# Down projections of an encoder trunk: eight pairs by Strassen's rule, and low parts of weights from an adding transfer

## The chip, the cores and the metric

The kernel runs on one core of one Trainium2 chip. Its time is the time on the device in microseconds (us), the median of several executions. A profile of one more execution shows what each engine did: TensorE (PE; its weight loads are PEld), VectorE (DVE), ScalarE (ACT), GpSimd (POOL), SyncE (SP, which only issues transfers here), and the 16 DMA engines.

## What is computed

A two-layer encoder trunk on 256 tokens of width 2048, in float32. Each layer is a token mixer (attention) and a gated channel mixer. Only the second one's last product is touched, the down projection, which takes 5632 channels back to 2048:

```python
D_MODEL, SEQ, D_FF = 2048, 256, 5632

def conv_glu(h, w_up, conv_w, conv_b, w_down):
    u = h @ w_up
    gate, val = u[..., :D_FF], u[..., D_FF:]
    gate = depthwise_conv3(gate, conv_w, conv_b)
    return (jax.nn.gelu(gate, approximate=False) * val) @ w_down

for i in range(2):
    h = rms_norm(x, p['mix_pre'])
    m = mixer_dilated_gqa(h, ...) if i == 0 else mixer_mla(h, ...)
    x = x + rms_norm(m, p['mix_post'])
    h = rms_norm(x, p['ffn_pre'])
    x = x + rms_norm(conv_glu(h, *p['ffn']), p['ffn_post'])
```

## The kernel before

**Products in three parts.** TensorE multiplies float32 in a rounded form (`F32R`). To keep float32's precision, each operand is split into a high part (the value rounded) and a low part (what the rounding lost), and each product is made of three: high by high, high by low, low by high. The weights are split on the way: a chunk of 128 x 1024 floats (512 KB; two blocks of 128 rows by 512 columns) is loaded by SP into a tile `raw` (four buffers), ACT copies it into `whi`, which rounds it (line 173), and DVE subtracts `whi` from `raw` into `wlo` (line 174). `whi` and `wlo` have three buffers each (lines 167, 168).

**The chunk planner.** All weights of the program stand in one list of chunks. `weights()` hands out the next chunk, splits the chunks up to two places further on (`i + 3` is the end of the range that is split, line 191), and issues the loads of up to three more. So a chunk's split is written into the program two chunks before its use, and its buffers come free when the chunk three places ahead of it has been multiplied. The recording layer then orders each engine's instructions itself; what stands on an engine is therefore shown below as rows of the built program.

**The down projection** (`down`, from line 1002 on) runs once for each layer, and covers the 2048 columns in two halves of 1024 (`h`). A half takes 22 pairs of 128-row blocks. A *plain* pair is two chunks, one for each 512 columns; a chunk is multiplied in 12 matmuls of 128 x 512: for each of the two groups of 128 tokens four with `whi` (lines 1101 and 1102) and then two with `wlo` (line 1104). A *Strassen* pair treats tokens, rows and columns as a 2 x 2 by 2 x 2 block product and needs seven products in place of eight, so 21 matmuls in place of 24. Its weights go through four items in place of two chunks: item 0 is the tile `seven_a` as loaded, then DVE makes four sums and differences of half tiles (`Seven.sums`, line 76) from `seven_a` and `seven_b`, which change `seven_a` and `seven_b` in place and write `seven_t`; items 1, 2 and 3 are the changed `seven_a`, `seven_b` and `seven_t` (the last is half as long). Each item is split on ACT and DVE as any chunk is. Items 0, 1 and 2 feed six matmuls each, item 3 three. `seven_a`, `seven_b` and `seven_t` have one buffer each, so the next pair's load waits until this pair's items are split.

**Order.** `down_order` sets the order of items in a half: some plain chunks ahead (`LEAD`: five in the first half, one in the second), then for each Strassen pair its four items with four plain chunks between them (item 0, plain, plain, item 1, plain, items 2 and 3, plain), and what is left of the plain chunks at the end. Sums of the tokens' side are made once for each layer by `sums()`, on DVE and ACT, and kept in `seven0` to `seven2`.

Of the kernel before, what the change touches and what calls it, by code (L numbers as in the profile page):

```python
# [9 lines left out]
F32 = mybir.dt.float32  # L10
F32R = mybir.dt.float32r
BF16 = mybir.dt.bfloat16
AF = mybir.ActivationFunctionType
ALU = mybir.AluOpType
AX = mybir.AxisListType

P = 128
# [7 lines left out]
EPS = 1e-6  # L25
NEG = -1e30
HOLD = 3
LAGS = 3, 2, 1

XM = 0, 1, 3, 2  # L30

PAIRS = 6
LEAD = 5, 1


def down_order(h):

    plain = [("plain", p, o) for o in range(2) for p in range(PAIRS, KF // 2)]  # L40
    out, plain = plain[:LEAD[h]], deque(plain[LEAD[h]:])
    for p in range(PAIRS):
        for j in (0, None, None, 1, None, 2, 3, None):
            out.append(plain.popleft() if j is None else ("seven", p, j))
    return out + list(plain)


class Seven:
# [5 lines left out]
    def __init__(self, a, b):  # L54
        self.srcs, self.raw = (a, b), None
# [31 lines left out]
class Model:  # L87
# [60 lines left out]
    def _load(self, i):  # L148
        if i >= len(self.chunks) or i in self.loaded or i < self.at or i in self.made:
            return  # L150
        if isinstance(self.chunks[i], tuple):
            self.chunks[i][0].load(self)
            self.loaded[i] = None
            return
        raw = self.wp.tile([P, 1024], F32, tag="raw", name="raw", bufs=4)
        self.nc.sync.dma_start(out=raw, in_=self.chunks[i])
        self.loaded[i] = raw

    def _split(self, i, parts=1):
        if i >= len(self.chunks) or i in self.made:  # L160
            return
        self._load(i)
        raw = self.loaded.pop(i)
        seven, step = self.chunks[i] if raw is None else (None, 0)
        if seven:
            raw = seven.step(self, step)
        hi = self.wp.tile([P, 1024], F32R, tag="whi", name="whi", bufs=3)
        lo = self.wp.tile([P, 1024], F32R, tag="wlo", name="wlo", bufs=3)
        n = raw.shape[-1] // parts
        with self.behind(self.gate):  # L170
            for j in range(parts):
                s = slice(n * j, n * j + n)
                self.nc.scalar.copy(hi[:, s], raw[:, s])  # L173
                self.nc.vector.tensor_tensor(out=lo[:, s], in0=raw[:, s], in1=hi[:, s].bitcast(F32),  # L174
                                             op=ALU.subtract)
        if seven and step == 0:
            seven.sums(self)
        self.made[i] = (hi, lo)
# [8 lines left out]
    def weights(self, upto=None):  # L187

        i = self.at
        if upto is None:  # L190
            upto = i + (2 if self.lead else 3)
            self.follow()
        for j in range(i, upto):
            self._split(j)
        for j in range(upto, i + 6):
            self._load(j) if j < upto + 4 else None
        self.at += 1
        return self.made.pop(i)
# [191 lines left out]
    def out_proj(self, nk, parts, post, pre, m3, order=None, before={}):  # L390
# [27 lines left out]
        part = self.three(ss)  # L418
        ps = self.proj_tok(nk, parts, order, hold=HOLD)
        m.append(room.tile([P, 2, 512], F32, tag=tag, name="m3", bufs=bufs))  # L420
# [103 lines left out]
    def attend(self, scores, sc, mask, v, v_gen, put, sp):  # L524
# [31 lines left out]
        for i in range(2):  # L556
            nc.vector.tensor_scalar(out=p[:, i, :], in0=p[:, i, :], scalar1=den[:, i:i + 1], scalar2=None,
                                    op0=ALU.mult)
        for _ in range(LAGS[0]):
            yield  # L560
# [9 lines left out]
        use["p"] -= 1  # L570
        for _ in range(LAGS[1]):
            yield
# [28 lines left out]
    def turned(self, sp, ps, n, block, tab, put, scale=None):  # L601
# [4 lines left out]
        for t in range(2):  # L606
# [25 lines left out]
            yield  # L632
        for _ in range(LAGS[2]):
            yield
# [367 lines left out]
    def down(self, gh, gl, post, pre):  # L1002

        nc = self.nc
# [3 lines left out]
        seven, m, gains = [], [], []  # L1008

        def sums():  # L1010

            for i in range(PAIRS // 2):
                tmp = self.act.tile([P, 2, 1024], F32, tag="xm3", name="sums")
                add(tmp[:, 0], gh[i].rearrange("p k t -> p (k t)").bitcast(F32),
                    gl[i].rearrange("p k t -> p (k t)").bitcast(F32))
                a = tmp[:, 0].rearrange("p (q k t f) -> p q k t f", q=2, k=2, t=2)
                s = tmp[:, 1].rearrange("p (q n f) -> p q n f", q=2, n=4)
                a11, a12, a21, a22 = (a[:, :, k, t] for t in range(2) for k in range(2))
                add(s[:, :, 0], a21, a22)
                add(s[:, :, 1], s[:, :, 0], a11, ALU.subtract)  # L1020
                add(s[:, :, 2], a11, a21, ALU.subtract)
                add(s[:, :, 3], a12, s[:, :, 1], ALU.subtract)
                yield
                seven.append(self.act.tile([P, 2, 4, 2, P], F32R, tag=f"xm{i}", name=f"seven{i}"))
                self.parted(seven[i][:, :, :, 0, :], seven[i][:, :, :, 1, :], s)
                yield

# [47 lines left out]

        gains.append(self.gain_row(post, 0))
        self.now(sums())
        ended = None
        for h in range(2):
            items = down_order(h)  # L1080
            units = [n for n, item in enumerate(items) if item[0] == "seven"]
            if h == 0:
                gains.append(self.gain_row(post, 1))
            n = len(items) - (HOLD if h else 0)
            todo = [(i, t) for i in range(n) for t in range(2)] + \
# [9 lines left out]
            def products(i, t, w):  # L1095
                group = []
                while used and used[0][1][:2] == (i, t):
                    q, (_, _, b, x, blk) = used.popleft()
                    group.append((banks[b], *x(), slice(512 * blk, 512 * blk + 512), q == first[b], q == last[b]))
                for bank, xh, xl, c, start, _ in group:  # L1100
                    mm(bank, xh, w[0][:, c], start=start, stop=False)  # L1101
                    mm(bank, xl, w[0][:, c], start=False, stop=False)  # L1102
                for bank, xh, _, c, _, stop in group:
                    mm(bank, xh, w[1][:, c], start=False, stop=stop)  # L1104

            for i in range(n):
                if i == units[0]:
                    banks += [self.psum("at") for _ in range(4)]
                w = self.weights()
# [17 lines left out]
        part = self.three(ss)  # L1127
        ws = [self.weights(self.at + HOLD - j) for j in range(HOLD)]
        for t in range(2):
            for j in range(HOLD):  # L1130
                products(n + j, t, ws[j])
# [24 lines left out]
    def all_chunks(self):  # L1156
        a = self.a
        groups = lambda w, gs: [w[g, c] for g in gs for c in range(w.shape[1])]
        out = groups(a["w_in0"], [8, 6, 7, 0, 2, 4, 1, 3, 5])
        out += [a["w_out0"][g, c] for g in range(4) for c in (4, 5, 6, 7, 0, 1, 2, 3)]  # L1160

        def down(w):
            items = []
            for h in range(2):
                pairs = [Seven(w[2 * h, p], w[2 * h + 1, p]) for p in range(PAIRS)]
                items += [w[2 * h + j, p] if kind == "plain" else (pairs[p], j) for kind, p, j in down_order(h)]
            return items

        ffn = lambda l: groups(a[f"w_up{l}"], [g for j in range(NFG) for g in (j, NFG + j)]) + \
            down(a[f"w_down{l}"])  # L1170
        out += ffn(0)
        out += groups(a["w_in1"], [0, 1]) + [a["w_kr"]]
        for p in range(8):
            out += groups(a["w_qr"], [p // 4]) if p % 4 == 0 else []
            out += [a["w_qn"][p], a["w_kn"][p]]
            out += groups(a["w_v"], [p // 2]) if p % 2 == 0 else []
        out += groups(a["w_out1"], range(4))
        out += ffn(1)
        return out
# [67 lines left out]
```

## Time and profile before

| | us |
|---|---|
| Median of 3 runs | 2062.15 (2062.04 to 2062.24) |
| Span of the profiled execution | 2060.1 |
| First to last matmul of layer 0's down projection | 822.75 to 1055.30 |
| The same for layer 1 | 1818.1 to 2050.6 |

The profiled execution's span runs from its first to its last instruction; the median of the runs, which is taken without the profiler, is 2.05 us above it. The two down projections are alike, 1020 matmuls and some 232.6 us each. In the groups of instructions and in the timeline, a row names the line, the engine, the operation and the tiles (what is written, an arrow, what is read); a matmul's duration is modelled and overlaps the next one, so the pace of matmuls is read from their starts.

### The profile page before, as it was taken

How to read it: one execution, taken by the hardware profiler on the slowest of the kernel's cores; microseconds unless marked ns; L12 is line 12 of the kernel's file. 1: busy time of each engine (PE TensorE's matmuls, PEld its weight loads, DVE VectorE, ACT ScalarE, POOL GpSimd, SP SyncE). 2: the span in 40 equal slices, each digit the busy share in tenths (PEclk: the TensorE clock that was granted, in tenths of full speed). 3: DMA queues.
4: the chain of work that ended last, by engine and by line, in shares of the span. 5: the costliest groups of instructions: out<-in, count | busy, mean ns of one | idle time of the engine just before them, and what ended most of it. 6: DMA issues, size and time to landing. Idle time of an engine off the chain costs nothing.

```text
span 2060.1 us, 29196 instructions
## 1 busy us (share of the span) xinstructions
PE 2043.4 (99%) x10905; PEld 1750.0 (85%) x10905; DVE 1478.4 (72%) x2263; ACT 1129.3 (55%) x1753; POOL 0.2 (0%) x4
## 2 busy tenths in 40 slices
PE   9999999999999999999999999999999999999998
PEld 7888888888888888888878998888888888888886
DVE  6877757766766767878787875676766766787877
ACT  6655546555555555555465664555555555554553
POOL 0000000000000000000000000000000000000000
PEclk9999999999999999999999999999999999999999
DMA  8545566666566666566655445566566566556664
GB/s 318 176 153 161 166 197 193 186 194 193 185 194 191 185 194 189 184 211 197 203 179 170 124 134 173 176 210 189 185 193 193 184 195 193 185 184 205 204 206 141
DMA packets 108717, 385.96 MB, mean 187 GB/s; under 512 B 12064, under 2 KB 12576, under 8 KB 108576
## 3 DMA queue, kind: packets, MB, share of 16 engines
q1 hardware_dynamic: 108288, 383.83, 59.3%
q8 instruction: 85, 1.39, 0.3%
q14 instruction: 56, 0.46, 0.1%
q10 hardware_dynamic: 288, 0.28, 0.0%
HBM read 381.96 MB, written 2.10 MB: 186 GB/s over the span
## 4 chain that ended last, share of the span: by engine, by line
PE 96%; DVE 3%; issue 0%; ACT 0%; DMA 0%; DVEq 0%; SPq 0%; ACTq 0%
PE ps L244 31%; PE ps L245 16%; PE ps L230 8%; PE ps L231 8%; PE ps L232 8%; PE ps L1104 7%; PE ps L1101 7%; PE ps L1102 7%; PE ps L537 1%; PE ps L300 1%; DVE x L454 1%; DVE wlo L174 1%; PE ps L478 0%; DVE sums L1005 0%; DMA raw<-in_w_in 0%
## 5 line engine op out<-in xcount | busy, mean ns | idle before, releaser
L174 DVE TENSOR_TENSOR wlo<-raw,whi 128x1024 fp32r<-128x1024 f32 (+1 forms) x662 | 807.6, 1221 | 490.3 <-ACT whi L173 487.6
L173 ACT CAST whi<-raw 128x1024 fp32r<-128x1024 f32 (+1 forms) x662 | 694.3, 1050 | 642.7 <-PE ps L244 302.4
L244 PE MATMUL ps<-xhl,whi 128*128 128x512 f32 x2816 | 978.7, 394 | 1.0 <-DVE xhl L591 1.0
L245 PE MATMUL ps<-xhl,wlo 128*128 128x256 f32 x2816 | 779.2, 277 | 0.0
L244 PEld LDWEIGHTS ps<-xhl,whi 128*128 128x128 f32 x2816 | 527.6, 188 | 123.1 <-DVE xhl L591 2.0
L245 PEld LDWEIGHTS ps<-xhl,wlo 128*128 128x128 f32 x2816 | 528.9, 188 | 1.0 <-DVE wlo L174 0.5
L1101 PE MATMUL ps<-whi,gh 128*128 128x512 f32 x584 | 227.3, 389 | 0.0
L1102 PE MATMUL ps<-whi,gl 128*128 128x512 f32 x584 | 227.2, 389 | 0.0
L1104 PE MATMUL ps<-wlo,gh 128*128 128x512 f32 x584 | 182.0, 390 | 0.8 <-DVE wlo L174 0.8
L230 PE MATMUL ps<-whi,xhl 128*128 128x512 f32 x352 | 138.7, 395 | 0.9 <-ACT whi L173 0.8
L231 PE MATMUL ps<-wlo,xhl 128*128 128x512 f32 x352 | 137.6, 391 | 0.0
L232 PE MATMUL ps<-whi,xhl 128*128 128x512 f32 x352 | 137.2, 390 | 0.0
L1104 PEld LDWEIGHTS ps<-wlo,gh 128*128 128x128 f32 x584 | 109.1, 188 | 25.2 <-DVE wlo L174 2.7
L1101 PEld LDWEIGHTS ps<-whi,gh 128*128 128x128 f32 x584 | 109.6, 188 | 22.8
L1102 PEld LDWEIGHTS ps<-whi,gl 128*128 128x128 f32 x584 | 109.6, 188 | 22.8
L230 PE MATMUL ps<-whi,oh 128*128 128x512 f32 x256 | 100.0, 390 | 0.0
L231 PE MATMUL ps<-wlo,oh 128*128 128x512 f32 x256 | 99.7, 389 | 0.0
L232 PE MATMUL ps<-whi,ol 128*128 128x512 f32 x256 | 99.6, 389 | 0.0
L305 ACT COPY half<-ps 128x256 f32<-128x256 f32 x176 | 65.1, 370 | 43.9 <-PE ps L244 34.6
L230 PEld LDWEIGHTS ps<-whi,xhl 128*128 128x128 f32 x352 | 66.0, 188 | 14.5 <-ACT whi L173 1.1
L232 PEld LDWEIGHTS ps<-whi,xhl 128*128 128x128 f32 x352 | 66.1, 188 | 13.9
L231 PEld LDWEIGHTS ps<-wlo,xhl 128*128 128x128 f32 x352 | 66.3, 188 | 13.4 <-DVE wlo L174 0.9
(211 smaller groups left out, 2061.0 us busy)
## 6 DMA issues: line engine op xcount, KB each, us to landing
raw<-in_w_up SPq DMA_DIRECT2D x352, 512.0 KB, 4.1
raw<-in_w_down SPq DMA_DIRECT2D x128, 512.0 KB, 3.9
raw<-in_w_in SPq DMA_DIRECT2D x88, 512.0 KB, 3.7
raw<-in_w_out SPq DMA_DIRECT2D x64, 512.0 KB, 4.1
seven_a<-in_w_down SPq DMA_DIRECT2D x24, 512.0 KB, 4.5
seven_b<-in_w_down SPq DMA_DIRECT2D x24, 512.0 KB, 4.2
gb<-in_post SPq DMA_DIRECT2D x16, 256.0 KB, 3.8
raw<-in_w_qn SPq DMA_DIRECT2D x8, 512.0 KB, 3.6
```

The source lines that it names most:

```text
L173: self.nc.scalar.copy(hi[:, s], raw[:, s])
L174: self.nc.vector.tensor_tensor(out=lo[:, s], in0=raw[:, s], in1=hi[:, s].bitcast(F32), op=ALU.subtract)
L230: mm(ps, lh, rh, start=start, stop=False)
L231: mm(ps, lh, rl, start=False, stop=False)
L232: mm(ps, ll, rh, start=False, stop=stop)
L244: mm(out[i], hi[:, s], x(k), start=k == 0, stop=False)
L245: mm(out[i][:, :T], lo[:, s], x(k)[:, :T], start=False, stop=k == nk - 1)
L300: self.tc.keep_in_program_order(self.nc.tensor.transpose(out, x, self.ident))
L305: self.nc.scalar.copy(b, ps[:, T:])
L1101: mm(bank, xh, w[0][:, c], start=start, stop=False)
L1102: mm(bank, xl, w[0][:, c], start=False, stop=False)
L1104: mm(bank, xh, w[1][:, c], start=False, stop=stop)
```

## The change

Eight pairs of the 22, no longer six, go by Strassen's rule (`PAIRS`), in both halves and both layers. With fewer plain chunks left, the order between the items is closer: pairs with an even number get two plain chunks between their items, pairs with an odd number three. The fourth tile of token sums, `seven3`, lives in the channel mixer's own pool.

Of the 28 plain chunks of a half, every second one up to the 24th (12 in all) is wrapped in `Summed`. For such a chunk ACT makes `whi` as before, and then writes its negative into `wlo`; a transfer issued by POOL then adds the chunk, read from HBM a second time, to what stands in `wlo`. DVE's subtraction falls away there. `whi` and `wlo` get four buffers, and `weights()` splits one chunk further ahead (`AHEAD`), in the whole program. The space that is set aside for transfers issued by POOL is cut to 1024 bytes a partition.

```diff
+AHEAD = 4
-PAIRS = 6
+PAIRS = 8
     for p in range(PAIRS):
-        for j in (0, None, None, 1, None, 2, 3, None):
+        for j in (0, None, None, 1, None, 2, 3) if p % 2 else (0, None, 1, None, 2, 3):
             out.append(plain.popleft() if j is None else ("seven", p, j))
+class Summed:
+    def __init__(self, src):
+        self.src = src
...
-        hi = self.wp.tile([P, 1024], F32R, tag="whi", name="whi", bufs=3)
-        lo = self.wp.tile([P, 1024], F32R, tag="wlo", name="wlo", bufs=3)
+        hi = self.wp.tile([P, 1024], F32R, tag="whi", name="whi", bufs=AHEAD)
+        lo = self.wp.tile([P, 1024], F32R, tag="wlo", name="wlo", bufs=AHEAD)
+        if isinstance(self.chunks[i], Summed):
+            with self.behind(self.gate):
+                self.nc.scalar.copy(hi, raw)
+                self.nc.scalar.activation(lo, hi.bitcast(F32), AF.Copy, scale=-1.0)
+            self.nc.gpsimd.dma_start(out=lo, in_=self.chunks[i].src, accum_op=ALU.add)
+            self.made[i] = (hi, lo)
+            return
...
-            upto = i + (2 if self.lead else 3)
+            upto = i + (2 if self.lead else AHEAD)
...
-                seven.append(self.act.tile([P, 2, 4, 2, P], F32R, tag=f"xm{i}", name=f"seven{i}"))
+                home, tag = (self.act, f"xm{i}") if i < 3 else (self.room, "seven3")
+                seven.append(home.tile([P, 2, 4, 2, P], F32R, tag=tag, name=f"seven{i}", bufs=1))
...
-                items += [w[2 * h + j, p] if kind == "plain" else (pairs[p], j) for kind, p, j in down_order(h)]
+                n = 0
+                for kind, p, j in down_order(h):
+                    n += kind == "plain"
+                    src = w[2 * h + j, p] if kind == "plain" else (pairs[p], j)
+                    items.append(Summed(src) if kind == "plain" and n % 2 == 0 and n < 25 else src)
-    nc = bacc.Bacc("TRN2", target_bir_lowering=False, num_devices=1)
+    nc = bacc.Bacc("TRN2", target_bir_lowering=False, num_devices=1,
+                   dynamic_dma_scratch_size=1024)
```

Three places show how the instructions stand now. In the changed file the lines of the split are 188 (`whi`) and 189 (`wlo`) for other chunks, 180 (`whi`), 181 (the negative) and 182 (the transfer) for a `Summed` one; the matmuls have lines 1117, 1118 and 1120.

The first place is ACT in the first half of layer 0, from one Strassen pair's item 0 to its item 3. Before:

```order
L173 CAST whi_8332<-seven_a_8292 128x1024
L173 CAST whi_8344<-raw_8306 128x1024
L173 CAST whi_8362<-raw_8324 128x1024
L173 CAST whi_8372<-seven_a_8292 128x1024
L173 CAST whi_8388<-raw_8348 128x1024
L173 CAST whi_8406<-seven_b_8294 128x1024
L173 CAST whi_8420<-seven_t_8336 128x512
```

Now, for the sixth pair (number 5):

```order
L188 CAST whi_8551<-seven_a_8523 128x1024
L180 CAST whi_8574<-raw_8543 128x1024
L188 CAST whi_8585<-raw_8560 128x1024
L181 ACTIVATE wlo_8575<-whi_8574 128x1024
L188 CAST whi_8594<-seven_a_8523 128x1024
L180 CAST whi_8604<-raw_8589 128x1024
L188 CAST whi_8621<-seven_b_8525 128x1024
L181 ACTIVATE wlo_8605<-whi_8604 128x1024
L188 CAST whi_8641<-seven_t_8555 128x512
```

ACT has two instructions more for two `Summed` chunks, and each negative stands behind the copy of the item that follows, not straight behind its own copy.

The second place is PE, around a plain chunk of the same stretch. Before:

```order
L1101 MATMUL ps_7996<-whi_8226,gh7_3116 128x512
L1102 MATMUL ps_7996<-whi_8226,gl7_3127 128x512
L1101 MATMUL ps_7996<-whi_8226,gh7_3116 128x512
L1102 MATMUL ps_7996<-whi_8226,gl7_3127 128x512
L1104 MATMUL ps_7996<-wlo_8227,gh7_3116 128x512 x2
L1101 MATMUL ps_7997<-whi_8226,gh7_3116 128x512
L1102 MATMUL ps_7997<-whi_8226,gl7_3127 128x512
L1101 MATMUL ps_7997<-whi_8226,gh7_3116 128x512
L1102 MATMUL ps_7997<-whi_8226,gl7_3127 128x512
L1104 MATMUL ps_7997<-wlo_8227,gh7_3116 128x512 x2
```

Now, for the `Summed` chunk in `whi_8574` and `wlo_8575`:

```order
L1120 MATMUL ps_8001<-wlo_8552,gh2_3111 128x512
L1117 MATMUL ps_8003<-whi_8574,gh5_3114 128x512
L1118 MATMUL ps_8003<-whi_8574,gl5_3125 128x512
L1117 MATMUL ps_8003<-whi_8574,gh5_3114 128x512
L1118 MATMUL ps_8003<-whi_8574,gl5_3125 128x512
L1117 MATMUL ps_8004<-whi_8574,gh5_3114 128x512
L1118 MATMUL ps_8004<-whi_8574,gl5_3125 128x512
L1117 MATMUL ps_8004<-whi_8574,gh5_3114 128x512
L1118 MATMUL ps_8004<-whi_8574,gl5_3125 128x512
L1120 MATMUL ps_8003<-wlo_8575,gh5_3114 128x512 x2
L1120 MATMUL ps_8004<-wlo_8575,gh5_3114 128x512 x2
L1117 MATMUL ps_8001<-whi_8585,gh6_3115 128x512
```

All eight matmuls with the high part now stand ahead of the four with the low part; for some other `Summed` chunks matmuls of the items that follow stand between the two groups as well.

The third place is DVE, over one Strassen pair. Before:

```order
L174 TENSOR_TENSOR wlo_8333<-seven_a_8292,whi_8332 128x1024
L174 TENSOR_TENSOR wlo_8345<-raw_8306,whi_8344 128x1024
L76 TENSOR_TENSOR seven_a_8292<-seven_b_8294,seven_a_8292 128x512
L76 TENSOR_TENSOR seven_t_8336<-seven_b_8294,seven_a_8292 128x512
L76 TENSOR_TENSOR seven_b_8294<-seven_b_8294 128x512
L76 TENSOR_TENSOR seven_a_8292<-seven_a_8292,seven_t_8336 128x512
L174 TENSOR_TENSOR wlo_8363<-raw_8324,whi_8362 128x1024
L174 TENSOR_TENSOR wlo_8373<-seven_a_8292,whi_8372 128x1024
```

Now, for the fourth pair (number 3):

```order
L189 TENSOR_TENSOR wlo_8368<-seven_a_8339,whi_8367 128x1024
L189 TENSOR_TENSOR wlo_8391<-raw_8359,whi_8390 128x1024
L83 TENSOR_TENSOR seven_a_8339<-seven_b_8341,seven_a_8339 128x512
L83 TENSOR_TENSOR seven_t_8371<-seven_b_8341,seven_a_8339 128x512
L83 TENSOR_TENSOR seven_b_8341<-seven_b_8341 128x512
L83 TENSOR_TENSOR seven_a_8339<-seven_a_8339,seven_t_8371 128x512
L189 TENSOR_TENSOR wlo_8411<-seven_a_8339,whi_8410 128x1024
```

One subtraction is gone from the row of work between a pair's item 0 and the end of its item 1; the rest stands as it stood.

More of the change, by code (lines that the diff above doesn't have):

```diff
@@ L155, in _load @@
         raw = self.wp.tile([P, 1024], F32, tag="raw", name="raw", bufs=4)
-        self.nc.sync.dma_start(out=raw, in_=self.chunks[i])
+        src = self.chunks[i]
+        self.nc.sync.dma_start(out=raw, in_=src.src if isinstance(src, Summed) else src)
         self.loaded[i] = raw
```

## The prediction

> **What bounds the kernel now.** The page first: its shares of busy time, and the chain that ended last.
>
> ```profile
> span 2060.1 us, 29196 instructions
> ...
> PE 2043.4 (99%) x10905; PEld 1750.0 (85%) x10905; DVE 1478.4 (72%) x2263; ACT 1129.3 (55%) x1753; POOL 0.2 (0%) x4
> ...
> PE 96%; DVE 3%; issue 0%; ACT 0%; DMA 0%; DVEq 0%; SPq 0%; ACTq 0%
> ```
>
> TensorE holds 96% of the chain, and POOL does nothing. So a matmul saved is time saved, as long as what feeds TensorE keeps up. A matmul's modelled duration overlaps the next one, so I take its pace from the windows of the two down projections, restricted to line 1101 (a third of their matmuls):
>
> ```profile
> core 0: us, PE busy (x) PEld busy (x), PEclk, DMA share, GB/s
> 822.70:1055.30 232.60, 132.41 (x340) 63.75 (x340) 1.00 0.62 196
> 1818.00:2050.60 232.60, 132.42 (x340) 63.76 (x340) 1.00 0.56 186
> ```
>
> Three lines of 340 make 1020 matmuls in 232.6 us, or 0.228 us each. How well it is fed shows in the waits at line 1104, which reads the low parts, over the whole span:
>
> ```profile
> its engine sat idle before it (us, times) until:
>   DVE wlo L174: 3.4, 8
> ```
>
> Eight waits of 3.4 us together: the split on ACT and DVE is nearly never late. The engines that make it, in layer 0's down projection (groups of instructions):
>
> ```profile
> L1102 PE MATMUL ps<-whi,gl 128*128 128x512 f32 x292 | 113.6, 389 | 0.0
> ...
> L174 DVE TENSOR_TENSOR wlo<-raw,whi 128x1024 fp32r<-128x1024 f32 x63 | 76.7, 1221 | 29.1 <-ACT whi L173 28.6
> L173 ACT CAST whi<-raw 128x1024 fp32r<-128x1024 f32 x63 | 66.1, 1052 | 59.6 <-PE ps L1102 58.3 <-DVE wlo L174 1.3
> ```
>
> ACT's copy (1.05 us) mostly waits for PE to let go of a buffer: the split runs as early as its buffers allow, not when its data comes. That makes a place's room a matter of buffers and of rows on PE.
>
> **What is saved.** Two more Strassen pairs in two halves of two layers, three matmuls each, are 24 matmuls: 24 x 0.228 = 5.5 us. DVE loses 48 subtractions and gains the sums and splits of the added pairs; ACT gains 48 negatives and six copies' worth of items a layer. By the windows they were busy for this long:
>
> ```profile
> 822.00:1056.00 234.00, 232.93 (x1026) 191.57 (x1024) 183.27 (x217) 121.64 (x140) 0.00 (x0) 1.00 0.62 196
> ```
>
> ACT stood at 121.6 us of 234 (the fourth number of engines, after DVE's 183.3); 24 negatives at 1.05 and six copies make it some 153, so neither engine becomes the bound by its sum. The splitting ahead by one more chunk in the rest of the program I count at nothing: PE is idle for only 16.7 us of the span in all, which bounds a gain, and a cost would have to come from loads that two more buffers don't delay.
>
> **What the adding transfer has to meet.** For a `Summed` chunk the low part comes in a row: copy, negative, transfer. None of it starts before the buffers of the chunk four places ahead are free. I count the room at the place that the change shows on ACT and PE (`wlo_8575`). ACT's negative stands behind the copy into `whi_8585`, whose buffer is that of the pair's item 2 (`whi_8519`). From the start of the last matmul on that buffer to the first on `wlo_8575` PE has 20 matmuls to start: that one, five more of items 2 and 3, six of item 0, and the eight high ones; 20 x 0.228 = 4.6 us. Of this go 0.39 us until that matmul ends (line 1102's 389 ns), the copy at ACT's pace, and the negative, for which the nearest row is the copy, 1.05 us. The pace and two other things are in the timeline of ACT, DVE and SP over one pair:
>
> ```profile
> 888.96 0.33 SPq L62 DMA_DIRECT2D seven_a<-in_w_down  x1
> ...
> 904.60 0.33 SPq L62 DMA_DIRECT2D seven_a<-in_w_down  x1
> ```
>
> ```profile
> 896.17 1.06 ACT L173 CAST whi<-seven_a 128x1024 fp32r<-128x1024 f32 x1 [0.31 <-PE ps L1102]
> 897.13 1.04 ACT L173 CAST whi<-raw 128x1024 fp32r<-128x1024 f32 x1
> ```
>
> ```profile
> 897.25 1.23 DVE L174 TENSOR_TENSOR wlo<-seven_a,whi 128x1024 fp32r<-128x1024 f32 x1
> 898.40 1.22 DVE L174 TENSOR_TENSOR wlo<-raw,whi 128x1024 fp32r<-128x1024 f32 x1
> ...
> 903.34 1.23 DVE L174 TENSOR_TENSOR wlo<-seven_a,whi 128x1024 fp32r<-128x1024 f32 x1
> ```
>
> Two copies in a row start 0.96 us apart. So 4.6 - 0.39 - 0.96 - 1.05 leaves 2.2 us for the transfer, from the negative's end to the first matmul on it. Counted in this way along the rows of PE and ACT (whichever is later: the buffer of `whi`, that of `wlo`, or the copy that stands ahead), the 24 transfers of a layer have this room: six 1.9 to 2.5 us (mean 2.2), seven 3.0 to 3.3 (3.2), seven 3.8 to 4.9 (4.4), four 5.7 to 6.8 (6.2). The narrow ones stand where short Strassen items lie between, or where a copy delays the negative.
>
> **How long the transfer takes** no row shows, since POOL issues none before. The nearest rows are SP's plain loads of the same 512 KB:
>
> ```profile
> q1 hardware_dynamic: 108288, 383.83, 59.3%
> ...
> raw<-in_w_down SPq DMA_DIRECT2D x128, 512.0 KB, 3.9
> ...
> seven_a<-in_w_down SPq DMA_DIRECT2D x24, 512.0 KB, 4.5
> ```
>
> A plain load lands 3.9 us after its issue. 59.3% of 2060.1 us for 383.83 MB is 1.67 us of all 16 DMA engines for 0.524 MB. An adding transfer reads the chunk and also what stands in `wlo`, so it is a load plus something: at least 3.9 us; with a second pass of 1.67 us through the engines 5.6; with a whole second trip 7.8. A time below 3.9 would need it to do more in less, and I see no reason for that. I take 5.6, since two streams have to be read but their latencies can overlap, and keep 3.9 and 7.8 for the range. What POOL itself needs to issue (SP needs 0.33 us) lies inside this spread, and so does the queueing: 24 transfers of one or two passes raise the share of DMA in a layer from 0.62 by 0.17 to 0.34.
>
> [...]
>
> **The sum.** PE waits for what a transfer takes beyond its room. In a layer at 5.6 us: 6 x 3.4 + 7 x 2.4 + 7 x 1.2 = 45.6 us. At 3.9: 6 x 1.7 + 7 x 0.7 = 15.1. At 7.8: 6 x 5.6 + 7 x 4.6 + 7 x 3.4 + 4 x 1.6 = 96. Twice that less 5.5 gives +85.7 (+24.7 to +186.5). Behind the waiting negative on ACT stand the next copies, but they wait for buffers that PE frees no sooner; behind POOL's transfer nothing stands but the next one. The profiled span would go from 2060.1 to 2145.8, and the median of the runs, 2.05 us above the span, from 2062.15 to **2148**.
>
> **Rivals.**
>
> *The Strassen pairs' own loop decides.* `seven_a` has one buffer. From the copy of item 0 (896.17) to the end of item 1's subtraction (903.34 + 1.23) take 8.4 us, only then the next load is issued (904.60), and it lands 4.5 us later: no pair can follow in less than 12.9 us. Before, PE needed 21 + 48 matmuls a pair, 15.7 us, and SP's two issues are 15.64 apart: PE set the pace, with 2.7 us in hand (888.96 + 4.5 to 896.17). Now it needs 21 + 24 or 21 + 36, 10.3 or 13.0 us. Seven loops are 90.3 us, against 4 x 10.3 + 3 x 13.0 = 80.2; less the 2.7 in hand PE waits 7.4 us a half, 30 in all: +24, **2086**. Where a `Summed` chunk stands behind item 0, a subtraction less (1.15 us) lies in the loop; three of seven so make it some 16 us, and **2073**. It decides if the transfer takes under some 3.9 us. At 5.6 it is covered: with 45.6 / 16 of waits a pair takes 14.4 us on average. For it: every duration in it is measured. Against: it needs a fast transfer.
>
> *Everything is hidden* (the other side). If the transfer takes under 2.5 us and the loop overlaps further than the rows let me see, the 24 matmuls are all that counts: 2062.15 - 5.5 = **2057**. The change gains as long as the waits stay below 2.7 us a layer, which needs transfers of some 2.5 us at most. For it: 3.4 us of waits in all before. Against: a plain load alone takes 3.9.
>
> *The clock falls in the waits.* The granted clock is 1.00 wherever PE works, and lower only once it has stopped:
>
> ```profile
> 2052.00:2061.00 9.00, 0.00 (x0) 0.00 (x0) 4.84 (x11) 0.60 (x3) 0.00 (x0) 0.57 0.51 198
> ```
>
> Here PE has no work, and the clock is 0.57. In the forecast the longest waits are 3.4 to 3.7 us. If each of the six longest of a layer were followed by 6 us at half the clock, that costs 3 us each, 36 in all: **2184**; with transfers of 7.8 us twenty waits of a layer would be long enough, and the time would be beyond 2260. [...]
>
> **How the numbers follow.** The forecast (waits for the low parts, transfers of 3.9 to 7.8 us) gets 0.75, the loop 0.11, everything hidden 0.06, the clock 0.08. The range of 8 in 10 reaches down into the loop's times, **2078**, and up to **2240**; left out are the hidden case, the fastest loop, and the slowest transfers and clocks. A measurement of this kernel can tell about 0.2% from no change, some 4 us: faster by more gets 0.05 (the hidden case without its remnants), within 0.01, slower 0.94.
>
> **What would show it.** Right: line 1120 idle before some 20 low parts of a layer, released by a transfer of POOL; transfers landing some 5.6 us after their issue; 275 us from first to last matmul of a down projection; 24 matmuls fewer. The loop instead: PE waiting at line 1117 for copies of `seven_a`, SP's issues of it 12 to 13 us apart, and low parts in time. Wrong: both projections near 230 us, or transfers that land within 2.5 us. The clock's rival would show in the windows as a granted clock below 1.00 while PE works.

## The result and the profile after

The changed kernel takes 2208.5 us (median of 6 runs, 2203.1 to 2212.6), the kernel before 2066.6 us beside it (6 runs, on two levels of 2062 and 2071 us). The ratio is 1.0689, with a 95% interval of 1.0667 to 1.0711: 142 us slower. The forecast was +86 us, 2148 us, in a range up to 2240. Below, a ratio is turned into us with 2062.

The page of the changed kernel, rows of the span, of busy time and of the chain that ended last:

```profile
span 2210.0 us, 29368 instructions
...
PE 2089.7 (95%) x10881; PEld 1775.5 (80%) x10881; DVE 1468.2 (66%) x2275; ACT 1186.7 (54%) x1819; POOL 42.1 (2%) x52
...
PE 5%; DMA 4%; issue 3%; DVE 1%; ACT 1%; DVEq 0%; ACTq 0%; POOLq 0%
```

TensorE issues 24 matmuls fewer (10905 before), and yet the span is 150 us longer. The shares of the chain add up to 14%: it could be followed back only through most of the second down projection. In that stretch transfers hold nearly as much of it as TensorE, where they held nothing before.

The windows of the two down projections, for matmuls of line 1117 alone (line 1101 before):

```profile
core 0: us, PE busy (x) PEld busy (x), PEclk, DMA share, GB/s
826.30:1130.60 304.30, 135.75 (x336) 66.31 (x336) 0.92 0.70 191
1895.20:2200.30 305.10, 137.40 (x336) 67.41 (x336) 0.90 0.68 181
```

Three lines of 336 are 1008 matmuls. They take 304.3 and 305.1 us, against 232.6 for 1020 before: 144 us more of the 150 by which the span grew, so nearly all of the loss lies here. The mean granted clock was 1.00 before, and is 0.92 and 0.90 now. The waits of the whole span that are released by POOL's transfer, on PE and on its weight loads, and three groups of PE:

```profile
PEld ps L1120 <- DMA wlo<-in_w_down: 115.7, 35, 6.2
...
PE ps L1120 <- DMA wlo<-in_w_down: 100.9, 34, 5.7
```

```profile
L1120 PE MATMUL ps<-wlo,gh 128*128 128x512 f32 x544 | 189.6, 438 | 100.9 <-DMA wlo<-in_w_down 100.9
...
L1117 PE MATMUL ps<-whi,gh 128*128 128x512 f32 x544 | 221.3, 407 | 0.5 <-DVE m L1020 0.5
...
L1117 PE MATMUL ps<-whi,seven 128*128 128x512 f32 x128 | 51.9, 405 | 0.3 <-ACT whi L188 0.3
```

Both engines name the same waits, so they are counted once: TensorE stood 34 times, 100.9 us in all and 5.7 at most, for a low part. At line 1117 with `seven`, where the loop of the Strassen pairs would show, it waited 0.3 us for copies, and 0.5 us elsewhere at that line. 1008 matmuls at 0.228 us are 229.8 us; two projections come to 459.6, with 100.9 of waits to 560.5, and 609.4 were measured. Most of the other 48.9 us are the clock's. In the two projections it stood at 0.50 in 19 stretches; their windows, summed:

```profile
sum 105.82, PE 81.56 PEld 64.54 DVE 42.06 ACT 28.86 POOL 11.19; mean PE 4.29 PEld 3.40 DVE 2.21 ACT 1.52 POOL 0.59
```

TensorE worked for 81.6 of these 105.8 us, and the rest lies inside the waits. Matmuls start 0.43 us apart there in place of 0.228 (870.80 and 871.23 us in the first stretch), so of the 81.6 some 38 us are lost. Some 5 us more belong to the waits: a wait is counted from the modelled end of the matmul ahead of it, 0.39 us after that one's start and so 0.16 us behind the pace, and there are 34. The last 6 us, the waits at line 1117 among them, are not broken down. The mean durations of 407 and 438 ns, where 389 and 390 stood, fit a slower clock.

The transfer itself: the page's issues, its DMA queues, the group of POOL, and what the trace says of line 182.

```profile
raw<-in_w_down SPq DMA_DIRECT2D x112, 512.0 KB, 4.4
...
wlo<-in_w_down POOLq DMA_DIRECT2D x48, 512.0 KB, 7.2
seven_a<-in_w_down SPq DMA_DIRECT2D x32, 512.0 KB, 4.7
```

```profile
q1 hardware_dynamic: 108288, 383.83, 56.2%
q0 software_dynamic: 6912, 25.17, 6.7%
```

```profile
L182 POOL DMA_DIRECT2D wlo<-in_w_down x48 | 41.9, 873 | 2135.6 <-DVE sums L1020 1607.0
```

```profile
DMA to landing us min/median/max: 5.5/7.2/9.4
```

It lands 7.2 us after its issue (median of 48), not 5.6. POOL's instruction is 0.87 us of that. By the share of the queues, 48 transfers took 6.7% of 2210 us of all 16 engines, 3.1 us each, and SP's loads of the same size 1.7 us (56.2% for 732 of 512 KB): the engine time of a second pass, as assumed.

One wait in the timeline of the changed kernel (other rows left out):

```profile
879.71 1.05 ACT L181 ACTIVATE wlo<-whi 128x1024 fp32r<-128x1024 f32 x1
...
881.12 0.86 POOL L182 DMA_DIRECT2D wlo<-in_w_down  x1 [20.24 <-ACT wlo L181]
...
883.81 0.39 PE L1120 MATMUL ps<-wlo,seven 128*128 128x512 f32 x1
...
886.90 1.06 ACT L181 ACTIVATE wlo<-whi 128x1024 fp32r<-128x1024 f32 x1
888.31 0.86 POOL L182 DMA_DIRECT2D wlo<-in_w_down  x1 [6.33 <-ACT wlo L181]
...
889.21 2.07 PE L1120 MATMUL ps<-wlo,gh 128*128 128x512 f32 x4 [5.01 <-DMA wlo<-in_w_down]
```

The negative ends at 880.76, POOL starts 0.36 us later, and TensorE wants the low part at 884.04, one pace after 883.81: a room of 3.3 us. The data is there 8.1 us after the issue, and TensorE has stood for 5.0. Meanwhile ACT and POOL have gone on to the next `Summed` chunk: its negative ends at 887.96, and its transfer starts at 888.31. The windows ahead of, at and behind this wait:

```profile
core 0: us, PE busy (x) PEld busy (x) DVE busy (x) ACT busy (x) POOL busy (x), PEclk, DMA share, GB/s
879.70:886.50 6.80, 4.50 (x20) 3.38 (x18) 3.41 (x4) 4.15 (x6) 0.86 (x1) 1.00 0.92 261
886.50:893.30 6.80, 4.09 (x10) 3.22 (x11) 4.32 (x6) 2.74 (x4) 0.86 (x1) 0.50 0.87 217
893.30:900.10 6.80, 6.80 (x32) 5.60 (x31) 3.48 (x4) 2.50 (x4) 0.00 (x0) 1.00 0.86 237
```

In the middle window the clock is 0.50. Its last 4.1 us have 10 matmuls; at full pace there would be 18. So this wait of 5 us costs some 2 us more behind it.

### The profile page after: what moved, and what is told of

It reads as the page before. It is cut to its first block, busy times and chain, and to the rows that moved or that the text cites. A ratio compares the mean times of both kernels' runs of the same rounds, so it can differ in the third digit from the quotient of the medians.

```text
span 2210.0 us, 29368 instructions
## 1 busy us (share of the span) xinstructions
PE 2089.7 (95%) x10881; PEld 1775.5 (80%) x10881; DVE 1468.2 (66%) x2275; ACT 1186.7 (54%) x1819; POOL 42.1 (2%) x52
## 3 DMA queue, kind: packets, MB, share of 16 engines
q1 hardware_dynamic: 108288, 383.83, 56.2%
## 5 line engine op out<-in xcount | busy, mean ns | idle before, releaser
L189 DVE TENSOR_TENSOR wlo<-raw,whi 128x1024 fp32r<-128x1024 f32 (+1 forms) x598 | 729.5, 1221 | 495.7 <-ACT whi L188 485.7
L188 ACT CAST whi<-raw 128x1024 fp32r<-128x1024 f32 (+1 forms) x598 | 626.8, 1050 | 566.4 <-PE ps L259 328.9
L1120 PE MATMUL ps<-wlo,gh 128*128 128x512 f32 x544 | 189.6, 438 | 100.9 <-DMA wlo<-in_w_down 100.9
L1117 PE MATMUL ps<-whi,gh 128*128 128x512 f32 x544 | 221.3, 407 | 0.5 <-DVE m L1020 0.5
L1118 PE MATMUL ps<-whi,gl 128*128 128x512 f32 x544 | 220.8, 406 | 0.0
L188 ACT CAST whi<-seven_a 128x1024 fp32r<-128x1024 f32 x64 | 67.2, 1050 | 146.7 <-DVE seven_a L83 75.0
L189 DVE TENSOR_TENSOR wlo<-seven_a,whi 128x1024 fp32r<-128x1024 f32 x64 | 78.3, 1224 | 97.5 <-ACT whi L188 95.7
L182 POOL DMA_DIRECT2D wlo<-in_w_down x48 | 41.9, 873 | 2135.6 <-DVE sums L1020 1607.0
```

The costliest lines, as they stand in the source:

```text
L182: self.nc.gpsimd.dma_start(out=lo, in_=self.chunks[i].src, accum_op=ALU.add)
```

## The experiments

In the table below "+" is time over the kernel before. The diffs are against the changed kernel.

**Pairs without transfers.** All plain chunks are split as before; the order, the eight pairs and the four buffers stay.

```
-                    items.append(Summed(src) if kind == "plain" and n % 2 == 0 and n < 25 else src)
+                    items.append(src)
```

> Eight Strassen pairs in the new order and four buffers, but no adding transfer: DVE subtracts as before. If the adding transfers make the loss, nearly all of the 142 us (6.9%) goes and PE no longer waits at the low parts. The Strassen pairs' own loop (12.9 us a pair against 10.3 or 13.0 of matmuls) would leave it 11 to 24 us above the kernel before, with waits at the high parts of seven_a; if the loop overlaps, it is 5.5 us below. If the closer order or the four buffers were the cause, more than 60 us of the loss would stay.

Measured: 2097.6 us, ratio 1.0150 (1.0120 to 1.0180), +31 us. Its waits of PE, and its down projections:

```profile
PE ps L1117 <- ACT whi L188: 22.1, 17, 2.5
```

```profile
824.80:1074.20 249.40, 133.78 (x336) 63.79 (x336) 0.99 0.57 183
1837.30:2086.40 249.10, 133.27 (x336) 63.34 (x336) 0.99 0.53 171
```

The transfers and what goes with them make 142 - 31 = 111 us, nearly four fifths. The pairs' own loop, the rival at +11 to +24, is real and dearer than worked out. Asked for the tile `seven_a` alone, the trace names the same waits:

```profile
  PE ps L1117: 22.1, 17
```

So TensorE waits at line 1117 for copies of `seven_a`, as that rival said. SP's issues of it stand 12.2 to 13.3 us apart early in layer 0 (six of them, 858.7 to 924.0), near the 12.9 that were worked out.

**Transfers without the two pairs.** Six pairs in the order of before, 48 adding transfers.

```
-PAIRS = 8
+PAIRS = 6
-        for j in (0, None, None, 1, None, 2, 3) if p % 2 else (0, None, 1, None, 2, 3):
+        for j in (0, None, None, 1, None, 2, 3, None):
```

> Six pairs in the old order, four buffers, and 12 adding transfers a half. If transfers that land 7 us after their issue are the cause, most of the loss stays: 80 to 140 us above the kernel before, with some 16 to 20 waits of 3 to 6 us a layer at the low parts, and the clock below 1.00 in the down projections. If the closely set pairs are the cause, it is within 20 us of the kernel before.

Measured: 2172.0 us, ratio 1.0506 (1.0460 to 1.0552), +104 us. The transfers alone cost most of it. 104 + 31 is 135 of the 142: the two halves of the change add up, although no wait for the loop shows at line 1117 when they are together. The closer order gives the transfers less room: TensorE waits 100.9 us for them there, and 71.9 us here.

**The four buffers alone.** Six pairs, the order of before and no transfer; only the splitting ahead by four is left (both edits above).

> Six pairs in the old order and no adding transfer: only the four buffers, the split one chunk further ahead and the smaller space for POOL's transfers. The prediction counts this at nothing: within 3 us of the kernel before. If it moves loads or splits for the worse elsewhere, it is 4 us or more above, with the loss ahead of the down projections.

Measured: 2062.3 us, ratio 1.0003 (0.9983 to 1.0023). Counted at nothing, and nothing shows.

**A plain transfer in the place of the adding one.** POOL copies the chunk over `wlo` instead of adding it. The low parts of those 48 chunks are then the weights themselves and not their remainder.

```
-            self.nc.gpsimd.dma_start(out=lo, in_=self.chunks[i].src, accum_op=ALU.add)
+            self.nc.gpsimd.dma_start(out=lo, in_=self.chunks[i].src)
```

> The changed kernel, but POOL's transfer copies the chunk over the low part's tile instead of adding to it, so the low parts of those chunks are not what the reference needs; order, buffers, waits and bytes from memory stay. If reading the second stream costs the time, the landing falls from 7.2 us to 5 or 5.8 (the engines' share from 3.1 us a transfer to 1.7) and the time falls by 40 to 70 us. If issuing through POOL costs it, the landing stays near 7 us and the time within 15 us of the changed kernel.

Measured: 2160.9 us, ratio 1.0451 (1.0406 to 1.0496), +93 us, so 49 us less than with the addition. Its queue, its landing, its waits:

```profile
q0 software_dynamic: 6912, 25.17, 3.7%
```

```profile
DMA to landing us min/median/max: 3.7/5.0/7.6
```

```profile
PE ps L1120 <- DMA wlo<-in_w_down: 62.9, 29, 5.6
```

3.7% of 2164 us for 48 transfers is 1.7 us of the engines each, SP's figure; the addition nearly doubles it, with as many packets and bytes in the queue, and lands 2.2 us later. Some 0.3 us of that is POOL's own instruction, 0.53 us here against 0.87. But a plain copy by POOL also takes 5.0 us, not the 3.9 of SP's loads from which the forecast started. Beside SP's loads, none of these 48 plain transfers by POOL landed in less than 3.7.

**The addition on DVE.** The same chunks, order and negatives on ACT, with DVE adding `raw` in place of the transfer.

```
-            self.nc.gpsimd.dma_start(out=lo, in_=self.chunks[i].src, accum_op=ALU.add)
+            self.nc.vector.tensor_tensor(out=lo, in0=raw, in1=lo.bitcast(F32), op=ALU.add)
```

> The changed kernel with ACT's negatives, but DVE adds the chunk from raw in place of the transfer. If the transfers' landing makes the loss, this is within 15 us of the kernel without them (e1), 25 to 45 us above the kernel before. If the negatives on ACT and the place they take in its queue are the cause, 80 us or more of the loss stays.

Measured: 2104.1 us, ratio 1.0195 (1.0162 to 1.0228), +40 us. That is some 9 us over the pairs alone, for ACT's negatives and the place of DVE's addition behind them, and the intervals of the two runs overlap (33 to 47 against 25 to 37). The other 102 of the 142 us come with the transfer.

**Five buffers for the transfers.** As the run of transfers without the two pairs, with `AHEAD = 5`.

> As the kernel with six pairs, the old order and 12 adding transfers a half, but with five buffers and the split one chunk further ahead, so that each transfer has some 2 us more room. If the room is what the landing of 7 us misses, the waits at the low parts fall to a third to a half: 20 to 65 us above the kernel before. If transfers slow the other loads or the engines as such, it stays within 20 us of the kernel with four buffers.

Measured: 2130.4 us, ratio 1.0316 (1.0266 to 1.0365), +65 us, against +104 with four. Waits, landing and windows with four buffers:

```profile
PE ps L1120 <- DMA wlo<-in_w_down: 71.9, 32, 4.5
```

```profile
DMA to landing us min/median/max: 5.4/7.5/10.1
```

```profile
825.00:1118.70 293.70, 138.88 (x340) 67.51 (x340) 0.93 0.71 197
1882.00:2166.10 284.10, 137.69 (x340) 67.25 (x340) 0.94 0.69 194
```

and with five:

```profile
PE ps L1120 <- DMA wlo<-in_w_down: 46.4, 34, 5.0
```

```profile
DMA to landing us min/median/max: 5.6/7.5/9.8
```

```profile
824.10:1088.60 264.50, 134.01 (x340) 64.97 (x340) 0.98 0.77 218
1852.80:2115.80 263.00, 133.40 (x340) 64.31 (x340) 0.99 0.74 207
```

The transfer is as slow as it was, 7.5 us; a buffer more gives it room. The waits fall by 25 us, to two thirds and not to the third or half that was expected, but the time falls by 39 and the projections by 50: the clock comes back from 0.93 and 0.94 to 0.98 and 0.99. There are about as many waits (34 against 32), shorter ones in the mean (1.4 us against 2.2, though the longest is 5.0), and far less time at half clock: TensorE worked in it for 70.6 us with four buffers and for 15.1 with five, which at 0.43 us in place of 0.228 is a loss of 33 and of 7 us. As many transfers, as slow as before, leave the clock up when TensorE stands less: in these two runs the clock is a cost of the waits, not of the transfers as such.

**TensorE kept busy.** 14 matmuls with zeros were put ahead of the low parts of each `Summed` chunk, to see the waits without the fall of the clock.

```
+                if t == 0 and isinstance(self.chunks[base + i], Summed):
+                    for _ in range(FILL):
+                        mm(group[0][0][:, :T], self.zeros[:, :P], self.zeros, start=False, stop=False)
```

> The changed kernel with 14 matmuls of zeros (some 1.6 us) put in front of the first matmul on an adding transfer's low part, so that TensorE idles less at a stretch; its time is not to be compared, since the zeros cost some where no wait covers them and the low parts stand earlier on PE. If it is idle time that lowers the clock, the time at half the clock falls from 117 us to below 60 and follows the idle stretches that are left above 3 us. If the transfers themselves lowered it, it stays above 100 us.

A single run: 2278.9 us. The time at half the clock stayed at some 113 us, where the first theory wanted less than 60. But the waits for the transfer were hardly less either (96.3 us, 31 of them, the longest 5.2): TensorE still stood idle, behind the zeros instead of ahead of them, and their own time came on top. So this settles nothing about the clock; the runs with four and with five buffers do.

**The loop of the pairs.** Five runs with eight pairs and no transfer. First two buffers each of `seven_a` and `seven_b`, and three of `whi` and `wlo` to make the space:

```
-AHEAD = 4
+AHEAD = 3
-                raw = model.room.tile([P, 1024], F32, tag=f"seven_{tag}", name=f"seven_{tag}", bufs=1)
+                raw = model.room.tile([P, 1024], F32, tag=f"seven_{tag}", name=f"seven_{tag}", bufs=2)
```

> Eight pairs in the new order, no adding transfer, three buffers as before, and two buffers in place of one for seven_a and seven_b, so that the next pair's load need not wait for this pair's last split. If the pairs' own loop over one buffer is what the kernel without transfers (1.5% above the one before) pays, its waits at line 1117 go and the 24 matmuls saved remain: 2 to 5.5 us below the kernel before. If the closer order pays in another way (ACT or DVE too late for items 1 to 3), it stays 10 to 30 us above.

Measured: 2081.8 us, ratio 1.0091 (1.0066 to 1.0117), +19 us. The waits for copies fall from 22.1 to 15.3 us (14 of them), so the single buffer seems to be part of the loop's cost and is not all of it; the three buffers of `whi` came with it and were not tried alone. The longest wait, early in layer 0's projection (DVE, ACT and PE; rows left out):

```profile
850.00 1.23 DVE L1020 TENSOR_TENSOR sums<-gh,gl 128x1024 f32<-128x1024 f32 x1
851.13 0.69 DVE L83 TENSOR_TENSOR seven_t<-seven_b,seven_a 128x512 f32<-128x512 f32 x1
851.73 1.10 DVE L1020 TENSOR_TENSOR sums<-sums 128x256 f32<-128x256 f32 x3
852.74 0.69 DVE L83 TENSOR_TENSOR seven_a<-seven_a,seven_t 128x512 f32<-128x512 f32 x1
...
853.55 1.05 ACT L188 CAST whi<-seven_a 128x1024 fp32r<-128x1024 f32 x1 [4.41 <-DVE seven_a L83]
...
854.64 0.79 PE L1117 MATMUL ps<-whi,seven 128*128 128x512 f32 x1 [3.74 <-ACT whi L188]
```

DVE does the sums of the tokens (line 1020) between the sums of the weights (line 83), and TensorE waits 3.7 us for the end of that row; the two rows of line 1020 are some 2.3 us of that work. The next two runs gave every pair three plain chunks, with four ahead of the first pair and none behind the last of half 0: once with these buffers, and once with one buffer of each `seven` and four of `whi`.

```
-LEAD = 5, 1
+LEAD = 4, 1
-        for j in (0, None, None, 1, None, 2, 3) if p % 2 else (0, None, 1, None, 2, 3):
+        for j in (0, None, None, 1, None, 2, 3):
```

> Eight pairs, no adding transfer, three buffers of whi and wlo, two buffers of seven_a and seven_b, as in the run with two buffers each (+19 us against the kernel before), but every pair now has three plain chunks between its items (13.0 us of matmuls) and none two (10.3 us), and half 0 is led by four plain chunks. Theory A, that what is left after doubling seven_a comes of the pairs that follow each other too closely for three buffers, above all the pairs of 10.3 us: the short waits at every second pair go, and at least half of the +19 with them; +3 to +10 us against the kernel before, 234 to 237 us a down projection. Theory B, that DVE's sums of the tokens at the start of the projection are what delays the copies: the one long wait of a layer stays (3.9 us and the half-clock stretch behind it), and the time stays within 4 us of +19. No loss at all (-5.5 us, the 24 matmuls saved) would need both gone.

> The even order of three plain chunks a pair and LEAD 4, with eight pairs, no adding transfer, four buffers of whi and wlo as in the changed kernel, and one buffer each of seven_a and seven_b. Theory A, the loop of seven_a with its one buffer (12.9 us from load to load by the trace of the kernel before): a pair now has 13.0 us of matmuls, so the loop just fits and the time falls from the +31 us of the pairs alone in the changed order to between -5 and +5 us against the kernel before. Theory B, loads and copies take longer in the closer order than in the kernel before (seven_b landed in 4.8 us against 4.5): each pair is late by about 0.5 to 1 us, 14 loops a layer, +10 to +25 us. A long wait near the token sums would show at the first two pairs of a layer.

Measured: 2091.4 us, ratio 1.0135 (1.0103 to 1.0167), +28; and 2108.0, ratio 1.0214 (1.0178 to 1.0249), +44. Both hopes fell: the even order is slower in either form. The waits of PE in the first say part of why:

```profile
PE ps L1117 <- DVE m L1020: 9.8, 2, 4.9
PE ps L1117 <- ACT whi L188: 7.7, 4, 3.4
```

The short waits at every second pair are gone, but twice TensorE now waits 4.9 us (up to 8.6 us with one buffer each) at the change of halves, where no plain chunk is left to cover the sums of the seven products into `m`. The projections explain only a part of the loss: they sum to 487.9 us against 484.8 in the old order, and with one buffer each to 498.6 against 498.5. The rest lies outside of them and stays open. The last two runs put three plain chunks behind each half again and took them from pairs 3, 5, 6 and 7 of half 0, with three buffers of `whi` and then with four (two of `seven_a`, one of `seven_b`, three of `raw`):

```
+        for j in (0, None, 1, None, 2, 3) if h == 0 and p in (3, 5, 6, 7) else (0, None, None, 1, None, 2, 3):
```

> As the run with two buffers each of seven_a and seven_b (+19 us against the kernel before, three buffers of whi and wlo), but half 1 has three plain chunks in every pair, and half 0 has two only in pairs 3, 5, 6 and 7, so that five plain chunks lead and three end each half as in the kernel before. Theory A, that the waits at every pair of two plain chunks come of its 10.3 us of matmuls being too few: the seven short waits of 0.8 us a layer fall to two or three, the long wait at the second pair of a layer goes or shrinks since the first pairs have more room, and the wait at the change of halves of the even order (5.2 us) does not come back since three plain chunks end each half; -3 to +8 us against the kernel before. Theory B, the long wait comes of the sums of the tokens on DVE and not of the pair's length: it stays at 3 to 4 us with its stretch of half clock, and the time is +10 to +16 us.

> The same order as the run with three plain chunks behind each half, with four buffers of whi and wlo, two of seven_a, one of seven_b and three of raw. Theory A, that a whi buffer is what the copy of seven_a lacks at the second pair: the wait there falls below 2 us and so does not bring the half clock; the time is -4 to +6 us against the kernel before. Theory B, that DVE's sums or the single seven_b decide: waits of 1 to 4 us remain at the pairs and the time is +10 to +25 us. Three buffers of raw instead of four could add waits at plain chunks, which would show as idle time released by copies of raw.

Measured: 2084.5 us, ratio 1.0085 (1.0057 to 1.0114), +17; and 2104.2, ratio 1.0179 (1.0141 to 1.0217), +37. The waits of PE in the one and in the other:

```profile
PE ps L1117 <- ACT whi L188: 13.7, 10, 4.3
```

```profile
PE ps L1117 <- ACT whi L188: 11.4, 10, 2.0
```

With three chunks behind each half the wait for `m` is gone (0.5 us are left in the second run). The long wait at an early pair stays at 4.3 us with three buffers, about as the theory of DVE's sums had it, and is 2.0 at most with a fourth (the clock is 0.99 in both projections of the one, 1.00 and 0.99 in those of the other). That suggests a part for the sums and one for the buffer, but `seven_b` and `raw` changed with it. The four-buffer version was slower all the same. In the profiles its two projections sum to 239.8 + 242.0 us by their first and last matmuls, no more than the 240.7 + 241.3 of the other, so the rest of its time lies outside of them. ACT's copies waited 30 us there for loads into `raw`, and 2 us in the other run, which points at the three buffers of `raw`; that was not tried by itself. None of these orders of eight pairs beat the kernel before, and none was found that does.

| run | + us (95%) |
|---|---|
| the change | 142 (138 to 147) |
| pairs without transfers | 31 (25 to 37) |
| transfers without the two pairs | 104 (95 to 114) |
| four buffers alone | 1 (-4 to 5) |
| plain transfer for the adding one | 93 (84 to 102) |
| DVE adds | 40 (33 to 47) |
| transfers, five buffers | 65 (55 to 75) |
| pairs, two buffers of each `seven` | 19 (14 to 24) |
| even order; with one buffer each | 28 (21 to 34); 44 (37 to 51) |
| three chunks behind each half; with four buffers | 17 (12 to 24); 37 (29 to 45) |

## Why the prediction was right, and where its size was off

**Direction and mechanism** were right. TensorE waits at line 1120 for POOL's transfers, in 34 of 48 places; taking the transfers out takes 111 of the 142 us away. Twenty places a layer were forecast and 17 are seen. A projection takes 304 to 305 us, where 275 were forecast; that the total still lies in the range owes much to the range's width and, below, to two errors that nearly cancel.

**The saving** was right: 24 matmuls fewer, and the sum of 1008 x 0.228 us holds to some 6 us of 609 once the waits and the clock are added.

**The length of the transfer**, 5.6 us, is the first term that was mis-sized: 7.2 were measured. The engine time of the second pass that it assumed is there, 3.1 us against 1.7. It began from SP's load, 3.9 us, where a plain transfer by POOL takes 5.0, and it gave the addition 1.7 us, where it adds 2.2.

**The rooms** were summed as if each stood alone. At 7.2 us the forecast's formula gives 6 x 5.0 + 7 x 4.0 + 7 x 2.8 + 4 x 1.0 = 81.6 us a layer; 50.5 were measured. That fits places which help each other: while TensorE waits for one transfer, ACT and POOL go on to the next. The trace bears it out. The place in the timeline above had 3.3 us, one of the rooms that were counted (3.0 to 3.3). The next one, whose negative ended while TensorE stood, had 10.3 us and no wait. Behind each of the ten waits of 4.7 us or more the next transfer had 5.5 to 10.3 us, and for nine of the ten TensorE did not wait. The half clock behind the long waits stretches these rooms too; no run separates the two. That the two errors, too short a transfer and too little room, nearly cancel (45.6 us a layer were forecast) is luck.

**The clock** is the term that made most of the difference. The forecast had it at nothing and set it aside as a rival with a chance of 0.08 and a price of 36 us; it came on top of the forecast, at some 38 us. With it and the 5 us that the count of the waits leaves out, 459.6 + 100.9 + 38 + 5 is some 604 of the 609.4. The forecast's longest waits were 3.4 to 3.7 us; with transfers of 7.2 us the longest are 5 to 6 (5.7 at most). The rival's 6 us at half the clock behind each of the twelve longest waits, and a length of wait that is long enough for it, are terms that no run shows: in the changed kernel the clock stood at 0.50 in 19 stretches, 5.6 us each in the mean, and the last section has a wait of 2.6 us with such a stretch behind it and one of 2.9 us without. The run with five buffers shows most plainly that the clock follows the waits: its 48 transfers land after 7.5 us as with four, the waits are 46.4 us in place of 71.9, and the clock is 0.98 and 0.99 in place of 0.93 and 0.94.

**The loop of the pairs** was said to be covered at 5.6 us, and to cost 11 to 24 us without the transfers. It costs 31 without them. The estimate knew of `seven_a`'s one buffer, and the loop is about as long as it said. It left out what two buffers do not mend; the runs point to DVE's sums of the tokens, the wait for `m` where no plain chunk covers it, and the clock (0.97 to 1.00 in the projections of these runs), and leave a part open. In the changed kernel it is covered in the sense that line 1117 hardly waits, but the closer order gives the transfers less room, and the sum of the halves shows that little was saved by it.

**Splitting ahead** was counted at nothing, and measured at 0.6 us (-4 to 5). ACT's 48 negatives were no bound; whether the 9 us of the run with DVE's addition are theirs is not clear of the noise.

## What to carry to other kernels

An addition in a transfer takes DVE's work away and puts a latency in its place, 7.2 us here: count the time from the last write of its target to the first read of its result, and ask for that many us of other work between them. Where TensorE is the bound, price a wait at its length and add the clock behind it, which did not go in proportion to the waits: here some 38 us on 100.9, and 7 on 46.4 with five buffers. Packing the costly items closer saves matmuls, but spends the rooms on which buffers, transfers and the sums of another engine live: here the 24 matmuls saved 5.5 us, and the kernel was 31 us slower all the same before any transfer was added.

## What the runs showed of the hardware

- An adding transfer of 512 KB issued by POOL took 3.1 us of all 16 DMA engines and landed after 7.2 us (5.5 to 9.4); the same transfer without the addition took 1.7 us and landed after 5.0 (3.7 to 7.6).
- In the two projections of the changed kernel the clock stood at 0.50 in 19 stretches, 105.8 us in all and 5.6 us each in the mean. Matmuls started 0.43 us apart there, and 0.23 us apart at 1.00.
- The length of a wait alone did not tell whether the clock fell. Ahead of the first stretch at 0.50 the wait is 2.6 us and ends at 869.36: TensorE is busy for 0.82 us of the 3.4 us in which it lies, still at 1.00, and then 8 matmuls, where 16 follow, fill 3.4 us at 0.50. The wait ahead of it was longer, 2.9 us up to 860.80, and the clock stayed at 1.00 through it and until 869.40 (first two rows). What set the two apart was not shown.

```profile
857.90:860.80 2.90, 0.00 (x1) 0.00 (x1) 2.51 (x6) 2.11 (x3) 0.79 (x1) 1.00 0.98 243
860.80:869.40 8.60, 6.02 (x26) 4.65 (x26) 4.04 (x4) 2.37 (x3) 0.08 (x1) 1.00 0.93 268
866.00:869.40 3.40, 0.82 (x5) 0.36 (x3) 0.98 (x1) 1.04 (x1) 0.00 (x0) 1.00 0.82 241
869.40:872.80 3.40, 3.40 (x8) 2.72 (x9) 0.24 (x1) 0.86 (x1) 0.00 (x0) 0.50 0.00 1
872.80:876.20 3.40, 3.40 (x16) 2.76 (x16) 3.15 (x5) 0.18 (x1) 0.00 (x0) 1.00 0.27 52
```
